# Hybrid encoder step on one core: another token order behind layer A, and no meta tokens in layer D's second half

## The chip, the cores and the metric

One NeuronCore of a Trainium2 chip runs the whole kernel. The metric is the device time of one execution in microseconds (us). Engines are named as in the profile: PE is TensorE (matmul), PEld its weight load, DVE is VectorE, ACT is ScalarE, POOL is GpSimd, SP is SyncE, which here only issues DMAs.

## The reference

A trunk of four layers with 1024 model features, on two token streams: a prompt of 272 tokens (16 meta tokens, then 256 frames) and a sample of 64 tokens with its own caches. Per layer:

```
u = rmsnorm(x, norm_pre[layer])
a: q, f, i, g = split(u @ w_in); gated linear recurrence in blocks of 16; y = (rmsnorm(o) * silu(g)) @ w_out
b: short causal convolution, two gates, linear scan;                     y = (h * silu(g)) @ w_out
c: latent attention, 16 heads; prompt: chunked causal mask on 272 keys;
   sample: 528 cached keys and its own 64;                              y = (o * silu(g)) @ w_out
d: a, b, g = split(u @ w_in); v = a * sigmoid(b)
   c = causal depthwise convolution of [history, v], 31 taps
   c = silu(layernorm(c));                                              y = (c * silu(g)) @ w_out
x = x + rmsnorm(y, norm_post[layer])
return yp[:, N_META:], ys, new states (among them D's last 30 values of v per stream)
```

The width inside the layers is 2048. The meta tokens' rows of the last x are not returned; their values in D's convolution input are needed, as history of the first 30 frames.

## The kernel before

Features lie on partitions, tokens on the free dimension. All 336 tokens are one operand: sample (64), meta (16), frames (256), in this order in every layer. An fp32 product is emulated: each operand is split into a high and a low part, and three matmuls (`mm3`, L397) add high x high, high x low, low x high. A tile of 128 output features over 1024 inputs (`in_tile`, L402) is 24 matmuls of 336 columns.

Weights come as 128x1024 slices of 512 KB on SP's DMA queue (L304), into three staging buffers. ScalarE copies the high part (`whi`, L323), VectorE, or GpSimd for the slices named in the list `PRM["lo"]`, subtracts it for the low part (`wlo`, L335). `tick` keeps this some slices ahead of the matmuls that use them.

Each engine runs its instructions in program order. That order is written by hand in the dictionary `PRM`: `"c"` orders the steps of layer C over the eight head pairs (`c_steps`, L94: a step with its lag in pairs; `"g"` is one gate tile); for layer D `"pump"` says how many of VectorE's taps are issued behind each tile, `"act"` the same for the scaled copies for GpSimd, `"g"`, `"tg"` and `"t"` where the 16 gate tiles (`dg`) stand and how much is pumped behind them, `"npm"` how many blocks of four taps of a tile's convolution TensorE does, `"ngt"` how many taps GpSimd adds (L1613, on copies that ScalarE scales, L1612); VectorE does the rest (L1621).

Layer A (38 to 335 us) works through 8 pairs of heads; `fin` (L928) norms and gates one head's output and splits it into `oh`, `ol`, the operand of the output projection. The residual x was loaded once at the start; layer A itself reads only its split.

Layer C (645 to 932 us) interleaves, per pair of heads p: gate tiles; queries (q0, q1); sample attention (`sqa`, `ssc`, `str`, `sol`, `sou`) over 592 keys; prompt attention per head: scores (`psc`), softmax (`pso`: maxima on DVE, exponentials on ACT L1450, scaling on DVE), transposes (`ptr`, L1458) and output (`pou`, L1474). The prompt is cut in meta (16), and two blocks of 128 frames. The transposed probabilities of the meta keys are a tile of 16 partitions (`ppm`, copied by DVE at L1471), those of the frames are `ppt` (copied by ACT). `p_out` is one matmul over 16 keys and 272 queries, one over 128 keys and 256 queries, one over 128 keys and 128 queries. Values (`values`, L1345) are made per four heads, as three tiles of 128 tokens.

Layer D (1009 to 1219 us) goes over 16 feature tiles j: tiles `db`, `da`, the gated v into `dext` with the history of each stream (604 columns: history, sample, zeros, prompt, ...), a round trip through DRAM (`store` and `shifts`) that gives four shifted copies for TensorE's taps, the convolution over 366 columns split over TensorE, GpSimd and VectorE, and sums `s1`, `s2` for the layer norm. Behind the loop stand the remaining gate tiles, the last two convolutions and g13; then the statistics (`mu`, `m2`: matmuls with `onesE`, PE waits there for POOL's last sum, L1640). Then norm, gates (L1753 on POOL) and the output projection (`outproj`, L583; x times `xr` on POOL at L599), and the last norm and y.

Of the kernel before, what the change touches and what calls it, by code (L numbers as in the profile page):

```python
# [22 lines left out]
NT = NS + NP  # L23
NMETA = 16
# [183 lines left out]
def constants():  # L208
    f = np.float32
    p = np.arange(128)  # L210
    pos = np.concatenate([NCACHE + np.arange(NS), np.arange(NP)]).astype(f)
# [8 lines left out]
    for h in range(2):  # L220
# [5 lines left out]
        "k_pair": np.ascontiguousarray(pm.reshape(128, -1)),  # L226
# [38 lines left out]
OUTS = {"y": (128, KD, NT), "hg": (2, 128, 16, 128), "rh": (128, 2, 16), "rc": (128, 2, 16, 3), "lat": (128, 2, NT),  # L265
# [3 lines left out]
def unpack(r):  # L269
    y = r["y"].transpose(1, 0, 2).reshape(D, NT).T  # L270
# [7 lines left out]
    s, p = slice(0, NS), slice(NS, NT)  # L278
    return tuple(c(z) for z in (
        y[NS + NMETA:][None], y[s][None], hg[1], hg[0], rh[1], rh[0], rc[1], rc[0],  # L280
        lat[p][None, None], lat[s][None, None], rope[p][None, None], rope[s][None, None], cc[1], cc[0]))
# [72 lines left out]
class Trunk:  # L354
# [47 lines left out]
    def in_tile(self, name, idx, tick=True):  # L402
# [10 lines left out]
        for k in range(KD):  # L413
            self.mm3(out[:, :NT], h[:, k], l[:, k], self.uh[:, k], self.ul[:, k], k == 0, k == KD - 1)
        if tick:
            self.w.tick()
        return out[:, :NT]
# [13 lines left out]
    def og_alloc(self, pool):  # L431
        self.oh = pool.tile([128, KE, NT], F32R, name="oh")
        self.ol = pool.tile([128, KE, NT], F32R, name="ol")
# [6 lines left out]
    def first_input(self):  # L440
# [78 lines left out]
        V.tensor_scalar(self.x1, ss[:, :NT], 1.0 / D, EPS, op0=OP.mult, op1=OP.add)  # L519
# [63 lines left out]
    def outproj(self, i, layer, ready, close):  # L583
# [6 lines left out]
        last = self.layers[-1] == layer  # L590
        accs = [self.acc() for _ in range(mp)]
        for g in range(KE // kg):
            hi, lo = self.w.get(layer + "o1", g)
            h, l = (z[:, :128 * mp * kg].rearrange("p (k c) -> p k c", k=kg) for z in (hi, lo))
            for kk in range(kg):
                k = g * kg + kk
                ready(k)
                if last and self.xr is not None and k % 2 == 0:
                    G.tensor_tensor(self.x[:, k // 2], self.x[:, k // 2], self.xr, op=OP.mult)  # L599
                for m in range(mp):  # L600
                    s = slice(128 * m, 128 * m + 128)
                    self.mm3(accs[m][:, :NT], h[:, kk, s], l[:, kk, s], self.oh[:, k], self.ol[:, k], k == 0, k == KE - 1)
# [3 lines left out]
        with ExitStack() as st:  # L606
            bp = self.pool(st, "bnd", 1)
            yg = bp.tile([128, KD, NT], F32, name="yg")
            sums = {n: bp.tile([128, NT], F32, name="sum" + n) for n in ("s" if last else "spq")}
            tail = {}  # L610

            def add(n, m, t):
                if m == 7:
                    tail[n] = t
                elif m:
                    V.tensor_tensor(sums[n], sums[n], t, op=OP.add)

            def new(n, m):
                return sums[n] if m == 0 else bp.tile([128, NT], F32, name="sq" + n)

            def evac(m, acc):
                s = new("s", m)
                A.activation(s, acc[:, :NT], AF.Square)
                g = self.col("npost", 8 * i + m)
                A.activation(yg[:, m], acc[:, :NT], AF.Identity, scale=g)
# [4 lines left out]
                A.activation(q, acc[:, :NT], AF.Square, scale=g)  # L630
# [10 lines left out]
            S = {n: ps.tile([128, 512], F32, name="S" + n)[:, :NT] for n in "sqp"}  # L641
# [3 lines left out]
            for m in range(mp, 8):  # L645
                acc = pa.tile([128, 512], F32, name="bacc")
                for g in range(2):
# [3 lines left out]
                    for kk in range(8):  # L651
                        k = 8 * g + kk
                        self.mm3(acc[:, :NT], h[:, kk], l[:, kk], self.oh[:, k], self.ol[:, k], k == 0, k == KE - 1)
# [9 lines left out]
            if last:  # L663
                l, r = self.nrm.tile([128, NT], F32, name="lnss", bufs=1), self.nrm.tile([128, NT], F32, name="rstd")
                A.activation(l, S["s"], AF.Ln, scale=1.0 / D, bias=self.eps)
            else:
                self.mm(S["p"], self.ones, sums["p"], True, False)
                for n in "qp":
                    self.mm(S[n], self.ones, tail[n], False, True)
# [3 lines left out]
                l, sq, t, w = (bp.tile([128, NT], F32, name=n) for n in ("lq", "sroot", "sst", "wz"))  # L673
# [21 lines left out]
            if last:  # L695
                pst = ExitStack()
                pf = self.pool(pst, "end", 2, PSUM)
                rp = pf.tile([128, 512], F32, name="rend", bufs=1)[:, :NT]
# [3 lines left out]
                def new_x(k, e):  # L702
                    t = yg[:, k] if e is G else pf.tile([128, 512], F32, name="yend")[:, :NT]
                    e.tensor_tensor(t, yg[:, k], r if e is G else rp, op=OP.mult)
                    e.tensor_tensor(self.x[:, k], self.x[:, k], t, op=OP.add)
                    nc.sync.dma_start(self.d["y"][:, k], self.x[:, k])
# [15 lines left out]
    def layer_a(self, i):  # L722
        nc, tc, V, A, G = self.nc, self.tc, self.V, self.A, self.G
        with ExitStack() as st0:
# [203 lines left out]
            def fin(u, t):  # L928
# [8 lines left out]
                V.tensor_tensor(n, n, s["sg"][:, t], op=OP.mult)  # L937
                self.split(self.oh[:, h], self.ol[:, h], n)
# [26 lines left out]
            for u in range(8):  # L965
                sg = wk.tile([128, 2, NT], F32, name="sg")
# [29 lines left out]
    def layer_b(self, i):  # L996
        nc, tc, V, A, G = self.nc, self.tc, self.V, self.A, self.G
        T = 340
        with ExitStack() as st0:
# [96 lines left out]
            def recur(n):  # L1096
# [7 lines left out]
                V.scalar_tensor_tensor(og[:, :, :NS], h[:, :, :NS], 0.5, s["sg"][:, :, :NS], op0=OP.mult, op1=OP.mult)  # L1104
                V.scalar_tensor_tensor(og[:, :, NS:], h[:, :, 67:339], 0.5, s["sg"][:, :, NS:], op0=OP.mult, op1=OP.mult)
# [11 lines left out]
            def xtile(n, t):  # L1117
# [5 lines left out]
                A.activation(e[:, t, 3:67], a[:, :NS], AF.Copy)  # L1123
                A.activation(e[:, t, 70:342], a[:, NS:], AF.Copy)
# [32 lines left out]
    def layer_c(self, i):  # L1157
        nc, tc, V, A, G = self.nc, self.tc, self.V, self.A, self.G
        NK = NCACHE + NS
        with ExitStack() as st:  # L1160
# [7 lines left out]
            def psum_pools(ps):  # L1168
# [10 lines left out]
            pm = cp.tile([128, 2, 64], F32, name="pm")  # L1179
# [3 lines left out]
            keyk = cp.tile([128, 5, 256], F32, name="keyk")  # L1183
            kps = wt.tile([128, NK], F32, name="kps")
            nc.gpsimd.dma_start(rp.rearrange("p a b -> p (a b)"), self.d["k_rope"])
            nc.gpsimd.dma_start(pm.rearrange("p a b -> p (a b)"), self.d["k_pair"])
            loads = [(keyt[:, l, a:b], self.d["ct"][:, l, c:d])
                     for l in range(2) for a, b, c, d in ((0, 512, 0, 512), (576, NK, 512, NCACHE))]
# [623 lines left out]
```

## Time and profile before

| | before |
|---|---|
| median of 3 runs | 1310.57 us (1309.44 to 1312.44) |
| profiled execution | 1316.76 us, its span 1315.0 us |
| granted TensorE clock, mean | 0.982 |
| PE busy | 1259.6 us (96%), 8402 matmuls |
| PEld busy | 1185.7 us (90%) |
| DVE busy | 893.1 us (68%) |
| ACT busy | 776.4 us (59%) |
| POOL busy | 290.4 us (22%) |
| DMA | 166.25 MB, mean 126 GB/s |

Busy is the time in which an engine has an instruction under way; matmuls overlap, so a start-to-start step is shorter than a matmul's own duration. The chain of waits follows the work that ended last back to the start: an engine's share in it is the time that the end waited for it. PEclk (and "granted") is TensorE's clock as a share of 2.4 GHz; 0.50 is the lower level, 1.2 GHz.

### The profile page before, as it was taken

To read this page: it belongs to the slowest core of one execution; us is meant where nothing else is said; L and a number is where in the kernel's file an instruction comes from. 1 tells how busy PE (TensorE), PEld (TensorE's weight loads), DVE (VectorE), ACT (ScalarE), POOL (GpSimd) and SP (SyncE) were. 2 spreads that over 40 slices of the span, in tenths; PEclk is the share of its full clock that TensorE was granted. 3 is DMA by queue.
4 is the path that set the end of the run, shared out by engine and by line. 5 is a ranking of instruction groups with operands and counts; after the bars stand their busy time and mean duration, and the time that the engine had idled before them with its cause. 6 is when DMAs were issued, how large, how long until landed. Compare 5 with 4: busy or idle time off the path is not lost.

```text
span 1315.0 us, 21810 instructions
## 1 busy us (share of the span) xinstructions
PE 1259.6 (96%) x8402; PEld 1185.7 (90%) x8402; DVE 893.1 (68%) x1654; ACT 776.4 (59%) x1448; POOL 290.4 (22%) x335
## 2 busy tenths in 40 slices
PE   8999999999999999899989999998999899999896
PEld 8999999999999999799879898887898789888795
DVE  5677666676658999957755555555657498886684
ACT  5677666667545877755554445444643756665563
POOL 0000000000001122100140000000002676878592
PEclk9999999999999999899989999899999899999999
DMA  6433343333441444344343222231242576767242
GB/s 211 142 124 92 125 126 107 131 126 104 137 145 66 145 145 145 113 147 144 110 158 105 88 89 81 67 99 60 91 150 71 165 199 179 208 178 196 77 139 74
DMA packets 58903, 166.25 MB, mean 126 GB/s; under 512 B 7616, under 2 KB 22048, under 8 KB 58800
## 3 DMA queue, kind: packets, MB, share of 16 engines
q1 hardware_dynamic: 55248, 157.28, 38.6%
q0 software_dynamic: 1504, 4.88, 1.2%
q10 hardware_dynamic: 2048, 2.70, 0.7%
q8 instruction: 66, 1.08, 0.3%
q14 instruction: 37, 0.30, 0.1%
HBM read 157.34 MB, written 7.50 MB: 125 GB/s over the span
## 4 chain that ended last, share of the span: by engine, by line
PE 71%; DVE 12%; ACT 6%; issue 3%; POOL 3%; DMA 2%; SPq 0%; ACTq 0%; DVEq 0%; POOLq 0%
PE acc L395 41%; PE bacc L395 9%; PE cv L395 3%; PE o L395 3%; PE hacc L395 3%; DVE wlo L335 2%; PE y L395 2%; PE sp L395 2%; ACT Pp L1450 2%; PE ss L395 2%; ACT whi L323 1%; PE misc L395 1%; DVE cv L1621 1%; POOL wlo L335 1%; DMA wraw<-in_wts_dram 1%
## 5 line engine op out<-in xcount | busy, mean ns | idle before, releaser
L395 PE MATMUL acc<-uh,whi 128*128 128x336 f32 x1208 | 390.5, 323 | 1.8 <-ACT vv L979 1.8
L395 PE MATMUL acc<-uh,wlo 128*128 128x336 f32 x1208 | 384.2, 318 | 0.0
L395 PE MATMUL acc<-ul,whi 128*128 128x336 f32 x1208 | 383.5, 317 | 0.0
L323 ACT ACTIVATE whi<-wraw 128x1024 fp32r<-128x1024 f32 (+2 forms) x263 | 269.0, 1028 | 91.2 <-DMA wraw<-in_wts_dram 64.0
L335 DVE TENSOR_TENSOR wlo<-wraw,whi 128x1024 fp32r<-128x1024 f32 (+2 forms) x233 | 286.1, 1243 | 25.2 <-ACT whi L323 24.7
L395 PEld LDWEIGHTS acc<-uh,whi 128*128 128x128 f32 x1208 | 228.8, 189 | 11.6 <-issue 5.0
L395 PEld LDWEIGHTS acc<-ul,whi 128*128 128x128 f32 x1208 | 228.9, 189 | 0.5 <-issue 0.2
L395 PEld LDWEIGHTS acc<-uh,wlo 128*128 128x128 f32 x1208 | 227.9, 189 | 0.0
L687 POOL TENSOR_TENSOR x<-x,sroot 128x336 f32<-128x336 f32 x6 | 5.3, 897 | 533.5 <-ACT sroot L675 390.6
L1621 DVE SCALAR_TENSOR_TENSOR cv<-dext,dw,cv 128x366 f32<-128x366 f32 x184 | 97.3, 594 | 3.5 <-PE cv L395 2.7
L1613 POOL TENSOR_TENSOR gp<-gp,gq 128x366 f32<-128x366 f32 x77 | 90.0, 1170 | 36.1 <-ACT gq L1612 32.2
L395 PE MATMUL bacc<-oh,whi 128*128 128x336 f32 x288 | 92.1, 320 | 0.0
L395 PE MATMUL bacc<-oh,wlo 128*128 128x336 f32 x288 | 91.3, 317 | 0.0
L395 PE MATMUL bacc<-ol,whi 128*128 128x336 f32 x288 | 91.1, 316 | 0.0
L335 POOL TENSOR_TENSOR wlo<-wraw,whi 128x1024 fp32r<-128x1024 f32 (+1 forms) x30 | 67.3, 2248 | 18.2 <-ACT whi L323 18.2
L395 PE MATMUL acc<-oh,whi 128*128 128x336 f32 x192 | 61.5, 320 | 1.9 <-ACT dsg L1665 1.1
L395 PE MATMUL acc<-ol,whi 128*128 128x336 f32 x192 | 61.1, 318 | 1.3 <-DVE ol L421 0.8
L395 PE MATMUL acc<-oh,wlo 128*128 128x336 f32 x192 | 60.9, 317 | 0.7 <-DVE wlo L335 0.7
L1450 ACT ACTIVATE Pp<-sp,mx 64x80 f32<-64x80 f32 (+4 forms) x80 | 30.0, 375 | 45.9 <-DVE mx L1448 26.0
L395 PEld LDWEIGHTS bacc<-ol,whi 128*128 128x128 f32 x288 | 54.2, 188 | 0.4
L395 PEld LDWEIGHTS bacc<-oh,whi 128*128 128x128 f32 x288 | 54.2, 188 | 0.4
L395 PEld LDWEIGHTS bacc<-oh,wlo 128*128 128x128 f32 x288 | 54.1, 188 | 0.0
(436 smaller groups left out, 2561.8 us busy)
## 6 DMA issues: line engine op xcount, KB each, us to landing
wraw<-in_wts_dram SPq DMA_DIRECT2D x243, 512.0 KB, 3.6
dsh<-dxt SPq DMA_DIRECT2D x60, 189.0 KB, 4.2
wraw<-in_wts_dram SPq DMA_DIRECT2D x16, 384.0 KB, 3.0
dxt<-dext SPq DMA_DIRECT2D x15, 198.0 KB, 4.1
out_hg_dram<-sf SPq DMA_DIRECT2D x16, 128.0 KB, 2.1
wraw<-in_wts_dram SPq DMA_DIRECT2D x8, 256.0 KB, 2.7
ukt<-in_ukt_dram POOLq DMA_DIRECT2D x8, 256.0 KB, 3.3
uv<-in_wts_dram POOLq DMA_DIRECT2D x8, 256.0 KB, 3.9
```

The source lines that it names most:

```text
L323: self.nc.scalar.activation(hi[:, :n], self.raw[i][:, :n], AF.Copy)
L335: e.tensor_tensor(lo[:, :n], self.raw.pop(i)[:, :n], hi[:, :n].bitcast(F32), op=OP.subtract)
L395: self.PE.matmul(out, l, r, start=start, stop=stop)
L687: G.tensor_tensor(self.x[:, k], self.x[:, k], sq, op=OP.mult)
L1450: A.activation(P[r0:r1, c:c + n], s[r0:r1, c:c + n], AF.Exp, scale=C_SCALE, bias=mx[r0:r1, j:j + 1], accum_out=sm[r0:r1, j:j + 1])
L1613: G.tensor_tensor(cv[j, "p"], cv[j, "p"], q, op=OP.add)
L1621: V.scalar_tensor_tensor(c[:, :T], ext[j % NX][:, n:n + T], tap(n, j), c[:, :T], op0=OP.mult, op1=OP.add)
```

## The change

- Up to layer A's recurrence the order stays sample, meta, frames. `fin` writes its output as meta, frames, sample, so that everything behind it has that order; x is loaded a second time from DRAM in the new order, by two DMAs on SP's queue at the third pair of heads of layer A (u == 2), and `x1` is written in two parts. Masks, positions and slices of B, C and D follow.
- Layer D's gate tiles, convolution outputs (366 to 350 columns), statistics, norm, output projection and y leave the 16 meta tokens out: 320 columns in place of 336. `db`, `da` and v keep 336.
- Layer C: the prompt is cut in 128, 128 and 16 tokens in place of 16, 128 and 128; the keys' tail is padded to 128 rows; `p_out` becomes three matmuls of 128 keys with 272, 192 and 64 queries; `p_tr`, the copies behind it and `qs` follow; `k_pair` is gone.
- `PRM`: another order of C's steps; in D one gate tile fewer in the loop and one fewer before the last convolution, so that two more stand behind it; one block of taps less on TensorE, one tap more on GpSimd and three on VectorE; 49 slices in place of 38 have their low part made by GpSimd (away: da 5, dg 9, dg 11, do1 14; new: fifteen, ten of them in C, five in D's loop).

```diff
     "c": ... (steps behind "str")
-     ["psc0", 0], ["pso0", 0], ["q1", -1], ["sol", 0], ["psc1", 0], ["k", -1], ["pso1", 0], ["ptr0", 0], ["g", [2]], ["pou1", 1]
+     ["g", [-2]], ["psc0", 0], ["pso0", 0], ["q1", -1], ["sol", 0], ["psc1", 0], ["g", [2]], ["k", -1], ["pso1", 0], ["ptr0", 0], ["pou1", 1]
-    "npm": [0, 2, 4, 3, 3, 2, 4, 3, 4, 4, 4, 4, 4, 4, 4, 3],
+    "npm": [0, 2, 4, 3, 3, 2, 4, 3, 4, 3, 4, 4, 4, 4, 4, 3],
-    "ngt": [5, 5, 2, 6, 4, 7, 4, 3, 7, 7, 9, 7, 3, 9, 1, 14],
+    "ngt": [3, 5, 2, 6, 6, 7, 4, 3, 7, 8, 8, 7, 2, 10, 1, 15],
-    "act": [1, 9, 6, 79, 2],
-    "pump": [[9, 8, 3, 0, 4], [6, 4, 6, 0, 6]],
-    "g": [0, 0, 0, 0, 1, 0, 1, 0, 2, 1, 1, 0, 1, 0, 1, 0],
-    "t": [2, 4, 14, 28],
+    "act": [0, 8, 7, 80, 2],
+    "pump": [[8, 6, 2, 0, 4], [4, 4, 6, 0, 5]],
+    "g": [0, 0, 0, 0, 1, 0, 1, 0, 2, 1, 1, 0, 1, 0, 0, 0],
+    "t": [6, 2, 22, 24],
-    "tg": [3, 2],
+    "tg": [2, 2],
...
# fin (layer A)
-                V.tensor_tensor(n, n, s["sg"][:, t], op=OP.mult)
-                self.split(self.oh[:, h], self.ol[:, h], n)
+                V.tensor_tensor(r[:, :NP], n[:, NS:], s["sg"][:, t, NS:], op=OP.mult)
+                V.tensor_tensor(r[:, NP:], n[:, :NS], s["sg"][:, t, :NS], op=OP.mult)
+                self.split(self.oh[:, h], self.ol[:, h], r)
...
             for u in range(8):
+                if u == 2:
+                    nc.sync.dma_start(self.x[:, :, :NP], self.d["x0"][:, :, NS:])
+                    nc.sync.dma_start(self.x[:, :, NP:], self.d["x0"][:, :, :NS])
...
# values
-                for j, (c, w) in enumerate(((0, 16), (16, 128), (144, 128))):
-                    a = self.acc()
-                    z = slice(c, c + 128)
+                G.memset(vt[:, 2], 0.0)
+                for j, (c, w) in enumerate(((0, 128), (128, 128), (256, 16))):
+                    a = self.acc()[:w]
+                    z = slice(c, c + w)
...
# p_tr
-                tr(a[:, 0:128], P[:, 16:144], self.ident)
-                tr(a[:, 128:256], P[:, 160:288], self.ident)
-                tr(a[:, 256:384], P[:, 288:416], self.ident)
-                tr(b[:16, 0:16], P[:16, 416:432], self.ident[:16, :16])
-                tr(b[:16, 16:144], P[:, 0:16], self.ident)
-                tr(b[:16, 144:272], P[:, 144:160], self.ident)
+                self.mm(a[:, 0:16], P[:, 416:544], self.ident[:, :16])
+                tr(a[:, 208:336], P[:, 400:528], self.ident)
+                tr(a[:, 16:144], P[:, 272:400], self.ident)
+                tr(a[:, 144:272], P[:, 0:128], self.ident)
+                tr(a[:, 336:464], P[:, 128:256], self.ident)
+                tr(b[:, :128], P[:, 256:384], self.ident)
-                A.activation(pt, a[:, :384], AF.Copy)
-                V.tensor_copy(pm_, b[:16, :NP])
+                A.activation(pt, a[:, :464], AF.Copy)
+                V.tensor_copy(pl[t][:16], b[:16, 64:128])
# p_out
-                self.mm(o[:, :NP], vt[:16, 0, z], pm_, True, False)
-                self.mm(o[:, 16:NP], vt[:, 1, z], pt[:, :256], False, False)
-                self.mm(o[:, 144:NP], vt[:, 2, z], pt[:, 256:], False, True)
+                self.mm(o[:, :NP], vt[:, 0, z], pt[:, :272], True, False)
+                self.mm(o[:, 80:NP], vt[:, 1, z], pt[:, 272:], False, False)
+                self.mm(o[:, 208:NP], vt[:, 2, z], pl[t], False, True)
...
# layer D
-        T = 366
+        T, M0, NQ, W = 350, NT - NL, NL - NS, 396
...
-                A.activation(sg[:, j], self.in_tile("dg", j), AF.Silu)
+                A.activation(sg[:, j], self.in_tile("dg", j, c0=M0), AF.Silu)
```

## Rows read from the trace of the kernel before

**Rows 1.** The page's chain of waits, shares of the span by engine.

```profile
PE 71%; DVE 12%; ACT 6%; issue 3%; POOL 3%; DMA 2%; SPq 0%; ACTq 0%; DVEq 0%; POOLq 0%
```

**Rows 2.** Windows: stretch, us, busy PE PEld DVE ACT POOL, PEclk, DMA, GB/s.

```profile
38.00:335.00 297.00, 296.54 (x2160) 291.85 (x2161) 196.61 (x429) 202.82 (x344) 0.00 (x0) 0.99 0.37 118
645.00:932.00 287.00, 271.93 (x1758) 246.82 (x1757) 155.65 (x377) 139.57 (x353) 28.56 (x47) 0.98 0.31 98
1078.00:1219.00 141.00, 140.90 (x1060) 121.16 (x1064) 113.89 (x191) 85.40 (x169) 112.34 (x89) 1.00 0.67 187
1227.00:1231.00 4.00, 3.98 (x9) 2.20 (x8) 0.00 (x0) 2.01 (x3) 2.20 (x2) 0.57 0.22 57
1236.00:1286.00 50.00, 47.66 (x304) 46.55 (x303) 42.82 (x53) 29.68 (x49) 44.86 (x32) 1.00 0.41 127
```

**Rows 3.** Timeline of TensorE, an attention output: start, us, line, tiles, count.

```profile
778.86 0.72 PE L395 MATMUL o<-ppm,vt 16*128 16x272 f32 x2
779.51 0.92 PE L395 MATMUL o<-ppt,vt 128*128 128x256 f32 x4
780.27 1.00 PE L395 MATMUL misc<-qn,ukt 128*128 128x64 f32 x8
```

**Rows 4.** Timeline of TensorE, last scores of a head and the transpose after them.

```profile
767.80 0.62 PE L395 MATMUL sp<-kp,qp 128*128 128x272 f32 x2
768.25 0.27 PE L1462 MATMUL pt<-ident,Pp 128*128 128x128 f32 x1
```

**Rows 5.** Timeline of TensorE, transposes of a head.

```profile
784.98 0.27 PE L1463 MATMUL pt<-ident,Pp 128*128 128x128 f32 x1
785.09 0.27 PE L1464 MATMUL pt<-ident,Pp 128*128 128x128 f32 x1
785.30 0.18 PE L1465 MATMUL misc<-ident,Pp 16*16 16x16 f32 x1
```

**Rows 6.** Waits of TensorE in layer C: total us, times, longest us.

```profile
PE sp L395 <- ACT Pp L1450: 4.0, 8, 2.1
PE misc L395 <- DVE ppm L1471: 1.8, 2, 0.9
```

**Rows 7.** The chain of waits in order of time: start us, us, what.

```profile
769.17 3.72 PE acc L395 x24
800.52 3.05 PE acc L395 x24
1145.25 2.60 PE cv L395 x32
```

**Rows 8.** Windows, the stretch of layer C with the lower clock.

```profile
841.80:848.60 6.80, 6.45 (x30) 5.94 (x29) 1.29 (x3) 0.87 (x2) 0.98 (x2) 0.50 0.43 151
```

**Rows 9.** Waits of TensorE, 1078 to 1240.

```profile
PE cv L395 <- POOL s L1640: 3.1, 1, 3.1
```

**Rows 10.** Groups of GpSimd by form: count, busy us, mean ns, idle before.

```profile
L1613 POOL TENSOR_TENSOR gp<-gp,gq 128x366 f32<-128x366 f32 x77 | 90.0, 1170 | 36.1 <-ACT gq L1612 32.2
L335 POOL TENSOR_TENSOR wlo<-wraw,whi 128x1024 fp32r<-128x1024 f32 x19 | 46.2, 2439 | 18.2 <-ACT whi L323 18.2
L335 POOL TENSOR_TENSOR wlo<-wraw,whi 128x768 fp32r<-128x768 f32 x11 | 21.1, 1918 | 0.0
L1753 POOL TENSOR_TENSOR dt<-dt,dsg 128x336 f32<-128x336 f32 x13 | 15.2, 1166 | 11.9 <-ACT dt L1750 11.9
L599 POOL TENSOR_TENSOR x<-x,xr 128x336 f32<-128x336 f32 x8 | 10.4, 1305 | 0.0
```

**Rows 11.** Windows, layer A where x's reload is put.

```profile
91.00:99.00 8.00, 8.00 (x65) 7.75 (x64) 4.00 (x7) 3.55 (x9) 0.00 (x0) 1.00 0.69 214
```

**Rows 12.** Timeline of ScalarE in layer A.

```profile
98.65 1.06 ACT L323 ACTIVATE whi<-wraw 128x1024 fp32r<-128x1024 f32 x1 [1.01 <-DMA wraw<-in_wts_dram]
103.27 0.47 ACT L875 ACTIVATE k<-x 128x384 f32<-128x384 f32 x1
```

**Rows 13.** Timeline of GpSimd in layer D.

```profile
1131.15 1.97 POOL L1613 TENSOR_TENSOR gp<-gp,gq 128x366 f32<-128x366 f32 x1
```

More of the change, by code (lines that the diff above doesn't have):

```diff
@@ L23 @@
 NT = NS + NP
+NL = NT - 16
 NMETA = 16
@@ L518, in first_input @@
         self.x1 = self.nrm.tile([128, NT], F32, name="x1", bufs=1)
-        V.tensor_scalar(self.x1, ss[:, :NT], 1.0 / D, EPS, op0=OP.mult, op1=OP.add)
+        for a, b in ((self.x1[:, :NP], ss[:, NS:NT]), (self.x1[:, NP:], ss[:, :NS])):
+            V.tensor_scalar(a, b, 1.0 / D, EPS, op0=OP.mult, op1=OP.add)
         w.ns = w.cur = 4
@@ L590, in outproj @@
         last = self.layers[-1] == layer
+        c0 = NT - NL if last else 0
+        n = NT - c0
+        X = [self.x[:, k, c0:] for k in range(KD)]
         accs = [self.acc() for _ in range(mp)]
@@ L607, in outproj, with add, new @@
             bp = self.pool(st, "bnd", 1)
-            yg = bp.tile([128, KD, NT], F32, name="yg")
-            sums = {n: bp.tile([128, NT], F32, name="sum" + n) for n in ("s" if last else "spq")}
+            yg = bp.tile([128, KD, n], F32, name="yg")
+            sums = {z: bp.tile([128, n], F32, name="sum" + z) for z in ("s" if last else "spq")}
             tail = {}
-            def add(n, m, t):
+            def add(z, m, t):
                 if m == 7:
-                    tail[n] = t
+                    tail[z] = t
                 elif m:
-                    V.tensor_tensor(sums[n], sums[n], t, op=OP.add)
-            def new(n, m):
-                return sums[n] if m == 0 else bp.tile([128, NT], F32, name="sq" + n)
+                    V.tensor_tensor(sums[z], sums[z], t, op=OP.add)
+            def new(z, m):
+                return sums[z] if m == 0 else bp.tile([128, n], F32, name="sq" + z)
             def evac(m, acc):
                 s = new("s", m)
-                A.activation(s, acc[:, :NT], AF.Square)
+                A.activation(s, acc[:, :n], AF.Square)
                 g = self.col("npost", 8 * i + m)
-                A.activation(yg[:, m], acc[:, :NT], AF.Identity, scale=g)
+                A.activation(yg[:, m], acc[:, :n], AF.Identity, scale=g)
                 add("s", m, s)
@@ L640, in outproj @@
             ps = self.pool(pst, "bnd_s", 1, PSUM)
-            S = {n: ps.tile([128, 512], F32, name="S" + n)[:, :NT] for n in "sqp"}
+            S = {z: ps.tile([128, 512], F32, name="S" + z)[:, :n] for z in "sqp"}
             if last:
@@ L667, in outproj @@
                 self.mm(S["p"], self.ones, sums["p"], True, False)
-                for n in "qp":
-                    self.mm(S[n], self.ones, tail[n], False, True)
-                l, sq, t, w = (bp.tile([128, NT], F32, name=n) for n in ("lq", "sroot", "sst", "wz"))
+                for z in "qp":
+                    self.mm(S[z], self.ones, tail[z], False, True)
+                l, sq, t, w = (bp.tile([128, NT], F32, name=z) for z in ("lq", "sroot", "sst", "wz"))
                 A.activation(l, S["s"], AF.Ln, scale=1.0 / D, bias=self.eps)
@@ L1279, in layer_c @@
             Pp = []
+            pl = [tm.tile([128, 64], F32, name=f"ppl{t}") for t in range(2)]
             for t in range(2):
-                z = tm.tile([128, 432], F32, name=f"Pp{t}")
+                G.memset(pl[t], 0.0)
+                z = tm.tile([128, 544], F32, name=f"Pp{t}")
                 G.memset(z, 0.0)
@@ L1327, in queries @@
                         qs = wk.tile([128, 2, 64], F32, name="qs")
-                        V.tensor_tensor(qs, qp[:, :NS].unsqueeze(1).to_broadcast([128, 2, 64]), pm, op=OP.mult)
+                        for h in range(2):
+                            V.tensor_scalar(qs[:, h], qp[:, NP:], self.col(f"m{h}"), None, op0=OP.mult)
                         Q[p].update(qp=qp, qs=qs)
@@ L1536, in layer_d @@
             ngt = lambda j: PRM["ngt"][j]
-            ext = [ep.tile([128, 604], F32, name=f"dext{j}") for j in range(NX)]
+            ext = [ep.tile([128, 460], F32, name=f"dext{j}") for j in range(NX)]
             for e in ext:
-                G.memset(e[:, 94:124], 0.0)
-            A.activation(ext[0][:, 0:30], dh[:, 0], AF.Copy, scale=2.0)
+                G.memset(e[:, :30], 0.0)
+            A.activation(ext[0][:, 302:332], dh[:, 0], AF.Copy, scale=2.0)
             dw = ep.tile([128, DTAP * 16], F32, name="dw")
@@ L1620, in conv_dve @@
                             continue
-                        V.scalar_tensor_tensor(c[:, :T], ext[j % NX][:, n:n + T], tap(n, j), c[:, :T], op0=OP.mult, op1=OP.add)
+                        V.scalar_tensor_tensor(c[:, :T], ext[j % NX][:, M0 + n:M0 + n + T], tap(n, j), c[:, :T], op0=OP.mult, op1=OP.add)
                         yield
@@ L1720, in layer_d @@
                 pump(PRM["t"][3])
-            g13 = self.in_tile("dg", 13, False)
+            g13 = self.in_tile("dg", 13, False, M0)
             pump(1000)
@@ L1724, in layer_d @@
             nc.sync.dma_start(self.d["cc"], cc)
-            mu, m2 = (pp["c"].tile([128, 512], F32, name="cv")[:, :NT] for _ in range(2))
+            mu, m2 = (pp["c"].tile([128, 512], F32, name="cv")[:, :NL] for _ in range(2))
             self.mm(mu, onesE, s1, True, False)
```

151 lines of the change are left out of this document (73 added, 78 removed), and 19 rows, old and new, of the table PRM.

## Prediction

> **What bounds the kernel now.** I read the chain of waits first: TensorE holds 71% of it [rows 1]. So the question for each edit is whether it shortens TensorE's own work or only the work of an engine that waits for it. The windows by stage come second [rows 2]. In layer A TensorE is busy for 296.54 of 297 us, in layer C for 271.93 of 287, in D's main loop for 140.90 of 141. In D's output projection it has 47.66 of 50 us with VectorE at 42.82 and GpSimd at 44.86, and the chain there runs over GpSimd's instructions, not over matmuls. Third come the timelines and the list of waits, for the places that are edited: attention in C, the gap ahead of D's statistics, and the weights that arrive around 98 us.
>
> The profiled execution took 1316.76 us (span 1315.0 and 1.8 around it), the median of the runs is 1310.57. The sum below is made against 1316.76 and then taken off the median, 6.2 us (0.5%) lower: every term is a piece of work, so it should be worth the same in either.
>
> **Layer C, attention output** (p_out, 16 heads). Before, a head's matmuls are one product with K=16 over 272 columns, one with K=128 over 256, one over 128; each fp32 product is two records. The two K=16 records take 0.65 us (778.86 to 779.51), the four others 0.76 [rows 3]. The same 272 columns with K=128 take 0.45 us for two records [rows 4] (767.80 to 768.25), 0.83 ns per column and record. After, it is 272, 192 and 64 columns, all K=128: 0.45 + 0.32 + 0.22 (the 64 columns at the 0.11 us that a 128-column record steps by, 784.98 to 785.09 in [rows 5]) = 0.99 us. That is 0.41 less, and the step from a full tile into a 16-row one costs 0.21 in place of 0.11 [rows 5] (785.09 to 785.30), so 0.1 more is gone: about 0.49 per head, 16 x 0.49 = **-7.8**. Bounds: -1.7 (only that step goes) and -8.2.
>
> The Trainium skill ("TensorE: Matmul & The Clock Gate", section "Why this matters for your kernels") states that a single K=32 matmul takes the same time as a K=128 one. By that rule only the dropped columns would count here, 1.7 us in place of 7.8 (rival 3). This trace does not agree: 0.65 us for K=16 [rows 3] against 0.45 for K=128 [rows 4], and I go by the rows.
>
> The rest of C. The values' last tile now has 16 stationary columns: entering and leaving it costs 2 x 0.1 us [rows 5] in each of the 4 quads of heads, **+0.8** (0 to 1.6). The transposes (p_tr) are six before and six after, one of them now an fp32 product of 16 columns: 0. Full-height keys (80 to 128 rows) remove one such tile change per product, at most 16 x 0.1 = 1.6; I take 0. The scalar copy grows from 384 to 464 columns and the vector copy shrinks to 16x64: neither engine is the bound in C, 0. The two qs operations replace one, behind a rope chain on VectorE: 0, with 8 x 0.2 if it is late.
>
> Against that stand the waits [rows 6]. TensorE waits 4.0 us in all for the exponentials (eight times, once per pair): a shorter TensorE waits as much longer where that chain ends last. It also waits twice, 0.9 each, for the vector copy queued behind a head's softmax, in pairs 4 and 6. In those two pairs the 2 x 0.49 saved ahead of the wait comes back: **+1.0**. Then the new order. The gate tile that stood after ptr0 now stands between psc1 and pso1. Its scalar square and vector multiply wait for its 24 matmuls (3.72 us, [rows 7]); queued behind them on VectorE are the maxima of head 1, then the softmax scaling and the copy out of the transposes, and TensorE's next attention output waits for that copy. That hits pair 2; price 0 to 3.7, I take the 0.9 of the like waits: **+0.9**. A stretch at half clock stands in C, 841.80 to 848.60 at granted 0.50 (1.2 GHz), after one of those 0.9 us waits [rows 8]. Of 6.45 busy us half, 3.2, would go if the clock stayed up, and 3.2 would come again at a second such wait. I take 0.
> C: -7.8 + 0.8 + 1.0 + 0.9 = **-5.1**, from -10.6 (-8.2, +0.8, and the half-clock stretch gone) to about 0.
>
> **Layer D up to the statistics.** 24 matmuls of 336 columns take 3.72 us, of 272 columns 3.05 [rows 7]: 0.43 ns per column, 6.9 ns for 16. Fourteen gate tiles lie on the path before the statistics: 14 x 24 x 6.9 ns = -2.3. A convolution's 32 records are 8 groups of four beside each other in 2.60 us: 0.325 us for 366 columns, 14 ns for 16, times 104 groups = -1.4; the eleven diagonal products of tile 0, -0.3; one block of four taps less on TensorE is a quarter of 2.60, -0.6. Together **-4.6**. Its three taps more on VectorE and one on GpSimd go beside it (113.89 and 112.34 of 141 busy).
>
> The gap. TensorE waits 3.1 us for GpSimd's last addition before the statistics [rows 9]. Before, only g13 follows conv_pe(15); after, two more gate tiles do, 7.1 us of matmuls in front of the same wait. The chain behind the last convolution (nine taps, finish, sums) is then covered: **-2.8**, from 0 (VectorE and GpSimd are late by as much as TensorE is earlier) to -3.1. With no idle ahead of it the half-clock stretch 1227 to 1231 (PEclk 0.57, 3.98 us busy, [rows 2]) could run at full speed, 3.98 x 0.43 = 1.7 less; behind it TensorE waits anyway for the scalar chain of the norm, so I take half, **-0.8** (0 to -1.7).
>
> **D's output projection** is bound by GpSimd. Its pieces [rows 10] are wlo slices of 1.92 us, gates of 1.17, the x products of 1.31. One of the slices (do1 14) goes to VectorE: -1.9. The 13 gates and 8 products sum to 25.6 us; 16 of 336 columns are 1.2, of which I take 0.8 since some of them stand beside waits. The final chain, twelve vector operations on 320 columns in place of 336, gives 0.4. **-3.1**, from -1 (VectorE, 42.82 of 50, takes the slice badly) to -4.5.
> D: -4.6 - 2.8 - 0.8 - 3.1 = **-11.3**.
>
> **Layer A, x reloaded.** Two transfers of 1.376 MB together now stand in SP's queue at about 91 us, ahead of the state load and the next weights. In 91 to 99 us the DMA engines moved 214 GB/s at a share of 0.69 [rows 11], that is 310 GB/s when full: 4.4 us. The weights landed at 98.6 and ScalarE was already waiting 1.0 us for them [rows 12]; 4.4 later, ScalarE starts that slice at about 103, and its copy of the transposed keys (103.27) moves to about 105.5. TensorE's state update follows that copy by about a microsecond and so waits 1 to 2 us: **+1.6**, from 0 (the transfers spread over the spare share and delay nothing) to 4.4 (the whole delay; the 64-token part goes in runs of 256 bytes, which could make it longer, and no row has the like). After that the three staged weights refill in the slack of the DMA share. The 16 vector multiplies split in two add 0.13 us each on VectorE, which is busy 196.61 of 297: 0.
>
> The ten slices moved to GpSimd in C and its output cost 2.44 us each [rows 10] on an engine that has 28.56 of 287 there [rows 2]; each is prepared two slices ahead of its matmuls: 0, and up to 2.4 us apiece if that lead is gone.
>
> **Sum:** -5.1 - 11.3 + 1.6 = -14.8. 1316.76 - 14.8 = 1302.0 for the execution as profiled; 1310.57 - 14.8 = 1295.8 for the median.
>
> **Rivals.** (1) C gives nothing: the softmax chain and a second half-clock stretch take back what p_out saves, and the reload costs its 4.4. For: 4.0 us of waits on exponentials exist already. Against: 13 of 16 heads have no wait behind p_out. -11.3 + 4.4 = -6.9, **1303.7**. (2) All comes through: C -10.6, D -13.0 (gap -3.1, clock -1.7, projection -3.6), reload hidden: -23.6, **1287.0**. For: the order was changed exactly where the waits stand. Against: the clock falls after waits shorter than a microsecond.
> (3) The long K=16 records come from what stands before and behind them, and the first product keeps that cost with K=128. At the rates of [rows 4] and [rows 5] p_out before would be 0.45 + 0.43 + 0.22 = 1.10 us, so it saves 0.11 per head, 1.7 in all; C's -5.1 becomes +1.0: -8.7, **1301.9**. For: the first record carries the step into the tile. Against: the second takes longer than 0.225 as well. It is the rule on K of the Trainium skill's page named above that gives this result.
> (4) Slower: GpSimd becomes the bound of D's main loop. It has 112.34 of 141 us; five slices join (da 4, 10, 13, db 15, dg 7) and three leave, +2 x 2.44 = +4.9, narrower tiles give -3.7: 113.5 of some 136. About 62 of its tap additions lie there at a mean of 1.17 [rows 10], yet single ones take 1.97 [rows 13]. If the mean rises over 1.17 + 22.5/62 = 1.53 us, GpSimd sets the loop; above 1.78 the other savings are gone. At 1.97 the loop is 27 us longer: 27.3 - 14.8 = +12.5, **1323**. For: it is busy for four fifths of the loop already. Against: nothing new shares its operands, and VectorE's share falls in the same windows.
>
> **How the numbers follow.** Forecast 0.52, rival 1 0.18, rival 2 0.18, rival 3 0.06, rival 4 0.06. The forecast's own range is 1290 to 1301. The range that leaves out 2 in 10 reaches to rivals 1 and 3 above and most of the way to rival 2 below: 1286 to 1305. A measurement of this kernel can tell 0.2%, 2.6 us, from no change: under 1308 is faster, above 1313.2 slower. Faster: the forecast, rivals 2 and 3, and most of rival 1, 0.91. Same: the upper end of rival 1, 0.04. Slower: rival 4 for the most part, 0.05.
>
> **What would show it.** Attention outputs of about 1.0 us in the chain where 1.50 stood; the 16-column values with steps of 0.2 at entry and exit; no wait of matmuls on GpSimd's sum before the statistics, two gate tiles behind the last convolution; gate tiles of 3.5 us; a wait for the reload's followers near 100 to 105 us in A. Wrong would be: a longer softmax wait in every pair, GpSimd continuously busy across D's loop, or weights landing late through more than one step of A.

## The result, and the profile after

The changed kernel takes 1292.57 us in the median (1291.13 to 1296.62), the kernel before 1310.01 beside it: a ratio of 0.9869, interval 0.9843 to 0.9895. A second set on the same code gave 0.9879 (0.9853 to 0.9904). The forecast was 1295.8, in a range of 1286 to 1305: faster, as expected, by 17.4 us where 14.8 was worked out. The two profiled executions, 1316.76 and 1296.62 us, differ by 20.1; the medians by 17.4.

The first lines to compare are the chain's shares. TensorE still holds most of the chain, less of it than before [rows 1]: the page of the changed kernel says

```profile
PE 65%; DVE 18%; ACT 7%; DMA 4%; issue 3%; POOL 1%; SPq 0%; ACTq 0%; DVEq 0%; POOLq 0%
```

Cut at the same matmuls of both traces (first tile of a layer, first product of the second part of an output projection, first convolution; the last row ends with VectorE's last instruction), the spans are (us):

| stretch | before | after | difference | other runs of the changed code there |
|---|---|---|---|---|
| head, layer A, first part of its output | 345.07 | 345.96 | +0.9 | 344.2 to 346.7 |
| second part of A's output, B, B's output | 296.82 | 296.12 | -0.7 | 296.1 to 298.3 |
| layer C, first part of its output | 304.90 | 296.29 | -8.6 | 294.6 to 297.0 |
| second part of C's output, D's first tiles | 79.98 | 81.20 | +1.2 | 79.9 to 81.3 |
| D's convolutions and tiles to the statistics | 199.86 | 192.10 | -7.8 | 190.2 to 192.2 |
| the statistics' products | 3.88 | 1.91 | -2.0 | 1.91 |
| norm and first part of D's projection | 55.70 | 53.26 | -2.4 | 53.2 |
| second part, last norm, y | 26.02 | 25.25 | -0.8 | 24.8 to 26.8 |

The windows of D, before and after (columns as in [rows 2]). They follow the same cuts, but the second one of the kernel before reaches 0.6 us into the projection:

```profile
1026.80:1226.60 199.80, 195.37 (x1398) 165.80 (x1398) 156.79 (x270) 121.02 (x241) 154.97 (x122) 0.98 0.67 185
1226.60:1231.15 4.55, 4.49 (x10) 2.64 (x11) 0.00 (x0) 2.32 (x4) 2.60 (x2) 0.62 0.23 64
1231.15:1286.20 55.05, 52.71 (x336) 51.60 (x336) 45.42 (x58) 33.83 (x55) 45.06 (x32) 1.00 0.38 117
```

```profile
1019.60:1211.70 192.10, 190.43 (x1391) 163.79 (x1392) 153.09 (x271) 121.70 (x244) 156.26 (x125) 0.98 0.65 185
1211.70:1213.60 1.90, 1.90 (x10) 1.34 (x9) 0.00 (x0) 0.23 (x2) 1.90 (x2) 1.00 0.00 0
1213.60:1266.80 53.20, 50.24 (x338) 49.37 (x337) 44.44 (x59) 33.77 (x56) 43.86 (x32) 1.00 0.44 143
```

In the first stretch TensorE's own time fell by 4.9 us and its idle time from 4.4 to 1.7. The statistics ran at granted 1.00 in place of 0.62. In the projection's windows TensorE's time fell by 2.5 us, GpSimd's by 1.2 and the stretch by 1.9; which of the two it follows is asked of an experiment below.

The waits of TensorE in C, which answer to [rows 6]:

```profile
PE sp L397 <- ACT Pp L1464: 3.9, 8, 2.1
PE misc L397 <- DVE ppl L1486: 3.5, 3, 1.3
PE acc L397 <- DVE sg L1212: 3.1, 1, 3.1
```

Two waits of 0.89 us on the vector copy became three: 0.81 at the third pair, where the gate tile was moved, and 1.32 at the fifth and seventh, where they had been. The third line was 2.0 before; that one was not foreseen, but it is no loss. In the profile before, the products ahead of this wait ran at granted 0.50 (664.3 to 667.7 us) and TensorE came to it later. In the run of the old code with 128 rows, below, they ran at full clock and the wait is 3.5. From the transposes of the latent keys (`kvr`) to the end of the wait stand 8.04 or 8.05 us in all three traces of the old code, and 7.62 in the changed kernel.

### The profile page after: what moved, and what is told of

Its sections match the earlier page's. It is cut to its first block, busy times and chain, and to the rows that moved or that the text cites. A ratio compares the mean times of both kernels' runs of the same rounds, so it can differ in the third digit from the quotient of the medians.

```text
span 1294.8 us, 21898 instructions
## 1 busy us (share of the span) xinstructions
PE 1237.7 (96%) x8410; PEld 1176.1 (91%) x8410; DVE 882.1 (68%) x1672; ACT 774.6 (60%) x1448; POOL 314.3 (24%) x353
## 4 chain that ended last, share of the span: by engine, by line
PE 65%; DVE 18%; ACT 7%; DMA 4%; issue 3%; POOL 1%; SPq 0%; ACTq 0%; DVEq 0%; POOLq 0%
PE acc L397 37%; PE bacc L397 9%; DVE wlo L337 4%; PE hacc L397 3%; PE cv L397 3%; PE o L397 2%; PE y L397 2%; PE sp L397 2%; ACT Pp L1464 2%; DMA wraw<-in_wts_dram 2%; PE ss L397 2%; DVE cv L1638 1%; DVE xc L1055 1%; PE misc L397 1%; ACT whi L325 1%
## 5 line engine op out<-in xcount | busy, mean ns | idle before, releaser
L397 PE MATMUL acc<-uh,whi 128*128 128x336 f32 (+1 forms) x1208 | 389.2, 322 | 5.8 <-DVE sg L1212 3.1
L397 PE MATMUL acc<-uh,wlo 128*128 128x336 f32 (+1 forms) x1208 | 382.9, 317 | 0.0
L397 PE MATMUL acc<-ul,whi 128*128 128x336 f32 (+1 forms) x1208 | 382.4, 317 | 0.0
L337 POOL TENSOR_TENSOR wlo<-wraw,whi 128x1024 fp32r<-128x1024 f32 (+2 forms) x41 | 95.0, 2322 | 130.8 <-ACT whi L325 85.1
L1638 DVE SCALAR_TENSOR_TENSOR cv<-dext,dw,cv 128x350 f32<-128x350 f32 x187 | 96.3, 580 | 0.9
L1630 POOL TENSOR_TENSOR gp<-gp,gq 128x350 f32<-128x350 f32 x78 | 87.2, 1121 | 26.6 <-ACT gq L1629 22.8
L397 PE MATMUL bacc<-oh,whi 128*128 128x336 f32 (+1 forms) x288 | 91.9, 319 | 0.0
L397 PE MATMUL bacc<-oh,wlo 128*128 128x336 f32 (+1 forms) x288 | 91.0, 316 | 0.0
L397 PE MATMUL bacc<-ol,whi 128*128 128x336 f32 (+1 forms) x288 | 90.9, 316 | 0.0
L397 PE MATMUL acc<-oh,whi 128*128 128x336 f32 (+1 forms) x192 | 61.0, 318 | 2.1 <-ACT dsg L1682 1.1
```

The costliest lines, as they stand in the source:

```text
L337: e.tensor_tensor(lo[:, :n], self.raw.pop(i)[:, :n], hi[:, :n].bitcast(F32), op=OP.subtract)
L397: self.PE.matmul(out, l, r, start=start, stop=stop)
L1630: G.tensor_tensor(cv[j, "p"], cv[j, "p"], q, op=OP.add)
L1638: V.scalar_tensor_tensor(c[:, :T], ext[j % NX][:, M0 + n:M0 + n + T], tap(n, j), c[:, :T], op0=OP.mult, op1=OP.add)
```

## The experiments

### Without the second load of x

```diff
-                    nc.sync.dma_start(self.x[:, :, :NP], self.d["x0"][:, :, NS:])
-                    nc.sync.dma_start(self.x[:, :, NP:], self.d["x0"][:, :, :NS])
```

> The changed kernel without the second load of x (so the residual behind layer A is in the old order). Theory 1, the weights behind the reload are late: ScalarE's slice that started at 101.5 us starts near 98, the third pair of heads in layer A is 1.1 us shorter (40.2 to 39.1), layer A 316.5 in place of 317.6 us, the whole about 1.1 below the changed kernel, near 1291.5. Rival, layer A is longer by the split write of its output alone: its length stays within 0.2 of 317.6 and the time at 1292.6.

Ratio 0.9851 (0.9827 to 0.9874); the time can't tell it from the changed kernel, the trace can. ScalarE in the changed kernel waits 4.4 us for the weights (1.0 before, [rows 12]):

```profile
101.48 1.06 ACT L325 ACTIVATE whi<-wraw 128x1024 fp32r<-128x1024 f32 x1 [4.44 <-DMA wraw<-in_wts_dram]
103.64 0.47 ACT L881 ACTIVATE k<-x 128x384 f32<-128x384 f32 x1
```

and without the load it starts the same slice with no wait, earlier than the 98 that was expected:

```profile
95.87 1.05 ACT L325 ACTIVATE whi<-wraw 128x1024 fp32r<-128x1024 f32 x1
101.61 0.47 ACT L881 ACTIVATE k<-x 128x384 f32<-128x384 f32 x1
```

The third pair of heads takes 40.03 us with the load and 39.08 without it (38.99 before). So the load costs 0.95 there. In six other executions with it, the pair took 39.85, 39.09, 39.88, 39.89, 39.24 and 40.52: 0 to 1.4 us, by how the transfers meet the weights. The 0.09 us that every pair gained also stands without the load: what differs there is the split write of A's output. That the two causes add is shown; that the split write makes the 0.09 is the remaining explanation and was not tried alone.

### K=16 in the last product of the attention output

```diff
-                self.mm(o[:, 208:NP], vt[:, 2, z], pl[t], False, True)
+                self.mm(o[:, 208:NP], vt[:16, 2, z], pl[t][:16], False, True)
```

> The changed kernel with K=16 in place of 128 in the last product of each attention output (64 columns, two records). Theory 1, a tile of 16 rows costs steps of its own: 0.1 us at entry and about 0.1 a record, 0.2 to 0.3 per head, 16 heads: +3 to +5, about 1296.5; the chain's attention output goes from 1.0 to 1.25 us. Rival, rows of the array cost nothing and only columns count: 0, 1292.6.

Ratio 0.9899 (0.9876 to 0.9922), 0.3% above the changed kernel; C takes 301.02 us in place of 296.29. One attention output in TensorE's timeline, which answers to [rows 3], first of the changed kernel, then of this one:

```profile
744.59 1.00 PE L397 MATMUL o<-ppt,vt 128*128 128x272 f32 x4
745.43 0.33 PE L397 MATMUL o<-ppl,vt 128*128 128x64 f32 x2
745.60 0.28 PE L397 MATMUL misc<-qn,ukt 128*128 128x64 f32 x1
```

```profile
744.69 1.00 PE L397 MATMUL o<-ppt,vt 128*128 128x272 f32 x4
745.62 0.43 PE L397 MATMUL o<-ppl,vt 16*128 16x64 f32 x2
745.98 0.32 PE L397 MATMUL misc<-qn,ukt 128*128 128x64 f32 x1
```

From the first record to the one behind: 1.01 us and 1.29 us, with the same columns. The 16-row records take twice their time (0.36 for the pair in place of 0.17) and the product in front of them is longer too (0.93 in place of 0.84). Added up over C, the attention outputs' steps are 21.87 us before, 15.88 after, 20.86 here: five of the six us that were gained come back with 16 rows on 64 columns alone. The step from the record ahead into an attention output comes on top. Before, it took 0.20 us into the 16-row record:

```profile
778.66 0.28 PE L395 MATMUL misc<-olat,uv 128*128 128x64 f32 x1
778.86 0.49 PE L395 MATMUL o<-ppm,vt 16*128 16x272 f32 x1
```

It takes 0.11 after, which is worth another 1.4 us over the 15 heads with no wait there. So 16-row records among 128-row ones cost time, and rival 3, by which they don't, falls. Whether the 16 rows themselves cost or the change from and to 128 rows is not shown: no run has 16 rows throughout.

### 128 rows in the first product of the kernel before

```diff
-                pm_ = tm.tile([16, NP], F32, name="ppm")
+                pm_ = pl                     # one tile of 128 rows, zeroed once
-                self.mm(o[:, :NP], vt[:16, 0, z], pm_, True, False)
+                self.mm(o[:, :NP], vt[:, 0, z], pm_, True, False)
```

> The kernel before with its 16 meta keys padded to 128 rows of zeros: K=128 in the first product of each attention output, the same 272, 256 and 128 columns. Theory 1: two records from 0.65 to 0.46 us and the step into the tile from 0.21 to 0.11, 0.3 per head, 16 heads: -4.7, less up to 1.2 where a wait behind it takes it back: 1305.3 to 1306.5. Rival (only columns count): 0, 1310.

1351.28 us, ratio 1.0297: neither, as a time. This version has one padded tile, which both heads share, and a head's probabilities are overwritten by the next ones before they are used. TensorE then waits for a copy that stands behind a softmax:

```profile
PE o L395 <- DVE ppl L1473: 31.8, 8, 6.1
```

So the time shows what a wait on that copy costs. What K costs is still to be read in the trace, at the attention outputs with no wait in front of them and at full clock:

```profile
750.81 0.28 PE L395 MATMUL misc<-olat,uv 128*128 128x64 f32 x1
750.92 0.68 PE L395 MATMUL o<-ppl,vt 128*128 128x272 f32 x2
751.43 0.82 PE L395 MATMUL o<-ppt,vt 128*128 128x256 f32 x4
752.09 1.00 PE L395 MATMUL misc<-qn,ukt 128*128 128x64 f32 x8
```

The first product takes 0.51 us in place of 0.65, the whole 1.17 in place of 1.41 [rows 3], on the same columns, and the step into it 0.11 in place of 0.20: together 0.33 per head, where theory 1 had 0.3. Only 0.06 above the 0.45 of [rows 4] stays with 128 rows. This is the second experiment against rival 3, on the old order of columns.

### The order of D's last gate tiles, on the kernel before

```diff
-    "g": [0, 0, 0, 0, 1, 0, 1, 0, 2, 1, 1, 0, 1, 0, 1, 0],
-    "t": [2, 4, 14, 28],
-    "tg": [3, 2],
+    "g": [0, 0, 0, 0, 1, 0, 1, 0, 2, 1, 1, 0, 1, 0, 0, 0],
+    "t": [6, 2, 22, 24],
+    "tg": [2, 2],
```

> The kernel before with the changed order of D's last gate tiles alone (two more behind the last convolution). Theory 1, the gap of 3.1 us before the statistics and their half-clock stretch (4.5 us in place of 1.9) both go: -5.7, 1304.3, no wait of matmuls on GpSimd's sum. Rival A, VectorE and GpSimd with the old widths are as late as before: gap shorter by less than 1, 1309 to 1310. Rival B, the last convolution, now 7 us earlier, waits for its shifted copies: a wait of 2 to 4 us on that transfer, 1307 to 1310.

Ratio 0.9967 (0.9953 to 0.9982): 4.3 us. The stretch to the statistics takes 196.90 in place of 199.86, the statistics 2.00 in place of 3.88, together 4.8 (5.7 was expected). Before them TensorE waits for nothing of GpSimd's; a new wait of 0.8 is there, on VectorE's taps:

```profile
PE cv L395 <- DVE cv L1621: 0.8, 1, 0.8
```

This is the theory; neither rival A (gap kept) nor B (late shifted copies, 2 to 4 us). It falls short of 5.7 mostly because 4.5 us for the old statistics was read in a window 0.6 us longer than they are (3.88).

### The old order of those tiles, on the changed kernel

The same diff, turned round.

> The changed kernel with the old order of D's last gate tiles (g, t, tg of before). Theory 1, as in the experiment on the kernel before: the gap before the statistics comes back, +2.5 to 3.5, and the statistics at half clock, +1.9: +4.4 to +5.4, 1297 to 1298, a wait of TensorE on GpSimd's sum. Rival, narrower tiles alone have closed the gap: within 1 of 1292.6.

The time, 0.9875 (0.9851 to 0.9899), does not show it; the trace does, at 3.0 us in all, less than the 4.4 to 5.4 expected. The waits ahead of the statistics, first of the changed kernel, then of this one:

```profile
PE cv L397 <- DMA dsh<-dxt: 1.6, 3, 0.9
```

```profile
PE cv L397 <- POOL s L1657: 2.1, 1, 2.1
PE cv L397 <- DMA dsh<-dxt: 1.9, 3, 1.1
```

The stretch takes 193.14 us in place of 190.55 (the run without the reload, as the nearest like it) and the statistics 2.30 in place of 1.91. A third of the gap (3.1 us before, 2.1 here) does not come back with the old order, and behind this wait the clock did not fall: granted 1.00 there. So the order and the rest of the change overlap: the order is worth 4.8 us on the old widths, 1.9 of them in the statistics, and about 3 on the new.

### Gate tiles on 336 columns

```diff
-                A.activation(sg[:, j], self.in_tile("dg", j, c0=M0), AF.Silu)
+                A.activation(sg[:, j], self.in_tile("dg", j)[:, M0:], AF.Silu)
```

> The changed kernel with layer D's gate tiles made on all 336 columns again (the 16 are left unread). Theory 1, TensorE's own columns: 15 or 16 tiles x 24 matmuls x 7 ns, +2.3 to +2.8 us, all of it in D's main loop and the tiles behind it: loop 193.0 in place of 190.5 us. Rival, D's loop is set by VectorE and GpSimd since the change: 0, 1292.6.

Ratio 0.9880 (0.9856 to 0.9904); the time can't tell it from the changed kernel. The stretch to the statistics takes 193.76 us in place of 192.10. Its window answers to the changed kernel's (192.10, 190.43 in the section on the result); the second line here is of the run without the reload, where the stretch takes 190.55:

```profile
1016.80:1210.50 193.70, 192.92 (x1390) 165.98 (x1391) 152.14 (x271) 122.03 (x244) 156.74 (x125) 0.98 0.66 184
```

```profile
1015.70:1206.20 190.50, 188.99 (x1390) 162.74 (x1391) 151.96 (x271) 121.69 (x244) 156.61 (x125) 0.99 0.67 187
```

The run without the reload is not like this one: the 22 diagonal products of tile 0 stand partly at half clock in all three, but for longer here and in the changed kernel (9.34 and 9.16 us of steps) than there (7.97). Against the changed kernel TensorE has 2.5 us more (192.92 for 190.43), 2.4 of it in the steps of D's input tiles, and its waits ahead of convolutions are 0.8 shorter (0.8 for 1.6): +1.7 us in all. VectorE and GpSimd change by less than 1 us. Theory 1 has the size of TensorE's own work right, but a third of it goes into waits that were there; the rival (those two engines set the loop, 0) falls.

### One low part back on GpSimd in D's projection

```diff
+          ["do1", 14]   (in "lo")
```

> The changed kernel with one more low part of the output projection (do1 14) back on GpSimd, as before the change. Theory of the prediction, GpSimd is the bound of the projection: +1.9 us, 53.3 to 55.2 us from the statistics to the second set of tiles. Rival, TensorE's own 288 matmuls are the bound there (50.3 us of steps in 53.3): 0, within 0.3 of 53.3.

Ratio 0.9879 (0.9852 to 0.9905). The projection's first part takes 54.22 in place of 53.24: between the two. TensorE's busy time is the same (50.54 for 50.24), and one wait is new, 0.74 us on a vector subtraction behind the late slice:

```profile
PE acc L397 <- DVE ol L1782: 1.5, 2, 0.8
PE acc L397 <- ACT dsg L1682: 1.1, 1, 1.1
PE acc L397 <- ACT dsg L1798: 1.0, 1, 1.0
```

The slice is late for one wait, but GpSimd is not the bound: 1.92 us of its work cost 1.0. Of the 2.4 us that the change gained here, the slice's move is thus about 1.0, and the rest goes with the narrower work.

### The gate tile of C put back

```diff
-          ["psc1", 0], ["g", [2]], ["k", -1], ["pso1", 0], ["ptr0", 0], ["pou1", 1]
+          ["psc1", 0], ["k", -1], ["pso1", 0], ["ptr0", 0], ["g", [2]], ["pou1", 1]
```

> The changed kernel with the gate tile of layer C that was moved ahead of head 1's softmax put back behind the transposes. Theory 1: the wait of 0.81 us at the third pair (776 us) goes, the two waits of 1.32 stay; C about -0.8, 295.0 in place of 295.8. Rival A, the tile comes too late for its other users and another wait of the same length takes its place: 0. Rival B, it takes all three waits away: -3.4.

Ratio 0.9866 (0.9839 to 0.9894). The waits in this stretch of C:

```profile
PE misc L397 <- DVE ppl L1486: 2.6, 2, 1.3
PE sp L397 <- ACT Pp L1464: 1.8, 7, 0.3
```

The 0.81 is gone, the two of 1.3 stay. From the third pair's wait for its exponentials to the fourth's stand 31.1 us in place of 32.1. C as a whole, 295.58, is not shorter than in the runs with the wait (294.6 to 297.0): 1.3 us were lost at its end in this execution, where matmuls behind the last 2.1 us wait ran at granted 0.77. In the changed kernel granted is 1.00 behind the same wait. So the change's own new wait costs 1.0 us, and an execution's clock can hide that.

### The control, and two versions meant to be faster

The control is the changed kernel once more.

> The changed kernel once more, as the control of the next two on the same chip: layer A's third pair 39.9 to 40.0 us, waits of 0.81, 1.32 and 1.32 us in C, D's main loop about 190.5 us; 1292 to 1296, ratio 0.986 to 0.988.

1297.19 us, ratio 0.9879 (0.9853 to 0.9904).

The next has C's gate tile as above, and x in four parts:

```diff
-                if u == 2:
-                    nc.sync.dma_start(self.x[:, :, :NP], self.d["x0"][:, :, NS:])
-                    nc.sync.dma_start(self.x[:, :, NP:], self.d["x0"][:, :, :NS])
+                if 2 <= u < 6:
+                    z = slice(2 * u - 4, 2 * u - 2)
+                    nc.sync.dma_start(self.x[:, z, :NP], self.d["x0"][:, z, NS:])
+                    nc.sync.dma_start(self.x[:, z, NP:], self.d["x0"][:, z, :NS])
```

> The changed kernel with x reloaded in four parts (two feature tiles at each of the pairs 2 to 5 of layer A) in place of one, and C's gate tile behind the transposes. Theory 1: 1.1 us of transfers at a time delay the weights by about 1 us, which the engines' slack covers: all pairs 39.1 us (-0.9), the wait of 0.81 in C gone (-0.9): -1.8 against the control. Rival: each part delays its pair by a quarter, and C's wait moves: 0.

1293.70 us (1291.07 to 1293.86), every run below the control's lowest (1295.97); ratio 0.9851 (0.9828 to 0.9873), the lowest of all with the run without the reload. Both parts do what was expected: all full pairs of A 39.06 to 39.10, the 0.81 gone. Against the control's profile, whose third pair took 40.52, that is 1.4 and 1.0, or 2.4 us. The other 1.1 of the 3.5 between the medians are not explained by the edits; ahead of the last matmul the control's profiled execution has nine half-clock stretches, this one three. ScalarE still waits at the place of the reload, and it costs nothing:

```profile
99.14 1.06 ACT L325 ACTIVATE whi<-wraw 128x1024 fp32r<-128x1024 f32 x1 [3.12 <-DMA wraw<-in_wts_dram]
```

The last one moves a gate tile from the first pair to the fifth.

```diff
-          ... ["g", [7]], ["g", [0]]
+          ... ["g", [7]], ["g", [4]]
```

> As the kernel with the reload in four parts, and one gate tile of C moved from the first pair to the fifth, behind its attention output. Theory 1, the wait of 1.3 us at the fifth pair is VectorE's copy queued behind a softmax, and a tile of 3.7 us in front of it covers it: that wait gone, -1.3 against the one before. Rival, the first pair loses the cover that the tile was: a new wait of 1 us or more there, 0.

1296.52 us, ratio 0.9885 (0.9862 to 0.9908), no gain. The rival: the wait at the fifth pair is gone and one of 2.4 us at the first pair is new.

```profile
PE misc L397 <- DVE ppl L1486: 3.8, 2, 2.4
```

## Why the prediction held, step by step

**That TensorE is the bound, and each saving counts in its own columns**: right in the main. D's stretches follow TensorE's column, but the gate-tile experiment moved the time by 1.7 us where TensorE's own work moved by 2.5: a wait on another engine or a transfer can take a third of a saving back.

**Attention output** (-7.8): mechanism right, and the size nearly. Its steps fell by 6.0 us and the steps into it by 1.4, 7.4 in all. The 0.99 us per head after the change was right (1.01 and 0.93 in turn), and so was the 0.1 for the step into the 16-row tile (0.20 to 0.11).

**Values with 16 columns** (+0.8): wrong. Their steps are 16.99 us before and 17.08 after. The step that [rows 5] show is that of a tile with 16 rows as well, and the price was carried over to one with 16 columns and 128 rows; 16 columns alone cost nothing here.

**Keys and transposes** (0): right. Their steps fell by 1.2 us (37.96 to 36.72, waits left out), but 0.65 of it are steps into attention outputs, counted above, and about 0.5 is the half clock of [rows 8], which covers one head's transposes.

**Waits in C** (+1.0 and +0.9): right in place and size, +0.87 and +0.81 (1.0 us of time by the experiment on that tile). The longer wait on a gate tile's vector product near the start of C, 2.0 to 3.1, is the clock's doing and costs nothing.

**Half clock in C** (0, with 3.2 either way): no other trace has the stretch [rows 8] at that place, leaving out the run with 128 rows, whose C is full of waits. In the kernel before with the new tail, granted is 1.00 there; laid beside that trace, matmul by matmul, the stretch cost 2.5 us. It belongs to that one execution, and goes some way to explain why the profiles differ by 20.1 and the medians by 17.4.

**Gate tiles, convolutions, one block of taps** (-2.3, -1.7, -0.6): right. Putting the gate tiles back cost 2.4 us of TensorE's steps, of which 1.7 show in the time. The convolutions with the block gave 2.4 of steps (43.67 to 41.24), as worked out, 0.5 of it in the diagonal products, where the clock has a part; no run changes them alone.

**The gap and the statistics** (-2.8 and -0.8): the gap is all gone, -3.1, and three short waits on shifted copies, 1.6 us together, stand where one of 1.4 stood. The statistics gave 2.0, above their bound of 1.7: that the scalar chain behind them would take half of it back was wrong.

**D's projection and tail** (-3.1): the size nearly right (-2.4 and -0.8), the reason wrong. I read the bound off the chain, which ran over GpSimd, while TensorE had 47.66 of 50 us [rows 2] and idle gaps of 2.3. One slice on GpSimd is worth 1.0, not 1.9; the rest goes with the narrower matmuls, of which TensorE has 2.5 us less. That the sum came out is in part luck: a slice priced too high stands for matmuls that were not priced.

**Reload of x** (+1.6): right in place, 0 to 1.4 in size. The two transfers landed 8.0 and 8.2 us after their issue, where 4.4 was worked out for both:

```profile
x<-in_x_dram SPq DMA_DIRECT2D x1, 1088.0 KB, 8.0
x<-in_x_dram SPq DMA_DIRECT2D x1, 256.0 KB, 8.2
```

Yet ScalarE started the late slice at 101.48 (about 103 was forecast) and the copy behind it at 103.64 (105.5): slack took most of the delay. What remains of layer A's longer pairs, 0.09 us each, put at 0, is most likely the split write.

**GpSimd as the bound of D's loop** (rival 4): it did not happen. GpSimd is busy for 156.26 of 192.1 us, 154.97 of 199.8 before, and no matmul waits for it there.

The profiled pair gives -20.1 where -14.8 was worked out. Of the 5.3 us more, C gave 3.5 (2.5 for the half clock, 0.7 for the values, less 0.4 for the attention output, the rest in small differences), the statistics 1.2, layer A 0.7, the stretch behind it, where nothing was forecast, 0.7, and D's convolutions 0.4; the stretch with D's first tiles took 1.2 back, by the clock.

## What to carry to other kernels

A share of columns left out is worth up to its columns where the engine that runs them is hardly ever idle: read that from the engine's busy time in the stretch, not from the engine that the chain names, and look at the waits that can take some of it back. Independent work issued ahead of a wait on a long chain is free cover; moving two tiles there was worth more than narrowing the gate tiles (3.0 and 1.7 us). A large transfer put into a queue of just-in-time weights should go in parts: in two runs four parts cost nothing, where one part cost 0 to 1.4 us in seven.

## What the runs showed of the hardware

The same program has stretches of half clock (1.2 GHz, matmuls of 336 columns stepping by 0.3 us) in different places from execution to execution: three to nine ahead of the last matmul in twelve of the thirteen traces, and eleven in the run whose attention outputs wait. All begin in a wait of TensorE of 0.8 us or more, or shortly behind one. But the same wait is followed by one in one execution and by full clock in another, as with the 2.1 us wait near the end of C (granted 0.77 and 1.00). The start of D's first tiles, behind a wait of 1.7 us, in the first profile of the changed kernel and in the run without the reload:

```profile
1000.90:1004.50 3.60, 3.59 (x14) 3.60 (x15) 3.46 (x8) 0.55 (x2) 0.00 (x0) 0.58 0.43 146
```

```profile
998.20:1004.00 5.80, 5.78 (x36) 5.49 (x37) 4.63 (x10) 0.97 (x2) 0.00 (x0) 1.00 0.28 90
```

The first is the +1.2 of that row in the table of stretches, in code that the change does not touch. One such stretch is worth 0 to 2.5 us here (0 where a longer wait stands behind it, 1.2 here, 2.5 at [rows 8]), as much as many of the edits. So an edit is better read from the step times and waits at its own place than from the time of one execution, and two traces may be set side by side only where their clock is alike.
